# Activation differences made one kind at a time and in place, and a re-ordered start of the second MLP matrix, in a float32 transformer layer on one core

## The chip, the cores and the metric

The kernel runs on one core of one Trainium2 chip. The metric is the device time of one execution in microseconds. TensorE (PE) multiplies, VectorE (DVE) and ScalarE (ACT) work on tiles in on-chip memory, GpSimd (POOL) and SyncE (SP) mainly issue DMAs. Each engine carries out its instructions in the order of its own queue, and waits on semaphores for the others.

## The reference

The layer is an attention and gating part, then a squared-ReLU MLP; the change touches the MLP alone. Sequence 512, model width 2048, hidden width 8192, all float32.

```python
h2 = rms_norm(x, g_ff[l])
x = x + jnp.square(jax.nn.relu(h2 @ w_ff1[l])) @ w_ff2[l]
```

## The kernel before

**Three products for one.** Every operand is split into a part `hi` (the value cast to the matmul's type, a CAST on ScalarE) and a part `lo` (the value minus `hi`, a subtraction on VectorE), and `mm3` (L71 to L73) multiplies hi by hi, lo and then lo by hi. `split_to` does it (L106 and L107).

**Seven products for eight.** Most of the MLP runs in Strassen's form. A block of weights has the quarters a = w11, w12, b = w21, w22; `Sums.parts` makes from them the left factors of seven products, named y11, y21, m7, m6, y22, m4, m5 (`NAMES`), by sums in place on VectorE (L172, L176, L178) and one accumulating DMA on POOL's queue that adds w22 onto w21 for m5 (L174). Each product's weights are then split into the pieces `w_hi` and `w_lo`, which share a ring of six buffers: a piece can be written when TensorE is done with the one that lay there. The right factors are the activations' quarters y11, y21, y22 and the differences m7 = y12 - y22, m6 = m7 - y11, m4 = y21 + m6, m5 = y11 - y12, which `factors` makes in slots of their own; `halves` splits each into a hi and a lo half of one slot (`ys`). The products are summed in four PSUM banks (`BANK`): y11, m6 and m5 share a bank, m7 and m4 share one, and y21 and y22 have their own. Of the shared ones, the later product adds onto what lies there, after ScalarE has copied the earlier state out (L722) into the pair's activations `relu`; VectorE adds the others (L725).

**First matrix, w_ff1.** The hidden width is walked in 32 pairs p of 2 x 128 columns. Pairs 0 and 1 (`PLAIN`) are done without Strassen; in pair 1 all 32 differences of the input (`hs`, eight k of four kinds) are made. Pairs 2 to 31 are `strassen_columns`: 7 products x 8 k x 3 = 168 matmuls of 128x256. After each pair `keep_hidden` squares its activations, makes the same seven kinds of the hidden activations and stores them in DRAM (seven DMAs of 256 KB on SP's queue, `store`). The squares of pairs 0, 1 and 2 are all kept after pair 2.

**Second matrix, w_ff2.** Eight chunks f of four pairs, each in two halves g of the output columns (`strassen_tokens`, two sets of weights i per half, 168 matmuls of 128x512). The kept activations come back by 28 `fetch` DMAs per chunk on POOL's queue, those of the next chunk asked for between the products. The result is added onto the residual `x2`, sixteen tiles of 256 KB that are read back from `kept` after the last pair.

**Order.** The program is written in this order, and a scheduler places each engine's instructions by its own estimate of when they can start; so an engine's queue isn't the order of the text. TensorE's order within a pair is y11, y21, m7, y22, m6, m4, m5, in both kernels. `behind` is a list of pieces of work; `step` runs the next one, `flush` the rest.

Of the kernel before, what the change touches and what calls it, by code (L numbers as in the profile page):

```python
# [9 lines left out]
F32 = mybir.dt.float32  # L10
# [24 lines left out]
def tile_hybrid_layer(ctx: ExitStack, tc: tile.TileContext, x, g_mix, w_in, g_q, g_k, ln_g, ln_b,  # L35
# [17 lines left out]
    def slot(name, dt=F32, pool=slots):  # L53
        return pool.tile([P, 512], dt, name=name, tag="slot")
# [103 lines left out]
    class Sums:  # L158


        def __init__(self, blocks, tiles):

            self.blocks = blocks
            self.w11, self.w12, self.w21, self.w22, self.a, self.c = tiles
            for t, hc in ((self.w11, (0, 0)), (self.w12, (1, 0)), (self.w21, (0, 1)), (self.w22, (1, 1))):
                state["load"] = nc.sync.dma_start(out=t, in_=blocks[hc])
            self.take = {"y11": self.w11, "y21": self.w12, "m7": self.a, "m6": self.c, "y22": self.w12,
                         "m4": self.w22, "m5": self.w21}

        def parts(self, name):  # L170
            if name == "m7":
                nc.vector.tensor_tensor(out=self.a, in0=self.w11, in1=self.w21, op=ALU.add)  # L172

                nc.gpsimd.dma_start(out=self.w21, in_=self.blocks[1, 1], accum_op=ALU.add)  # L174
            if name == "m6":
                nc.vector.tensor_tensor(out=self.c, in0=self.a, in1=self.w22, op=ALU.add)  # L176
            if name == "y22":
                nc.vector.tensor_tensor(out=self.w12, in0=self.c, in1=self.w12, op=ALU.add)  # L178
            src = self.take[name]
            hi, lo = piece("w_hi"), piece("w_lo")  # L180
            like = "p (k c) -> p k c"
            hi, lo = (t.rearrange(like, k=src.shape[1]) for t in (hi, lo))
            split_to(hi, lo, src)
            return hi, lo

    def strassen_columns(wap, c0, rhs, evac):
# [4 lines left out]
        w = Sums(blocks, [state["raw"].tile([P, KH, P], F32, name="w_raw", tag="w_raw") for _ in range(6)])  # L191
# [12 lines left out]
    def strassen_tokens(wap, r0, c0, lhs, evac, between):  # L204

        KQ = 2
        ws = []
        for i in range(2):
            rows = wap[r0 + i * 2 * KQ * P:r0 + (i + 1) * 2 * KQ * P, :]
            blocks = {(h, c): rows[:, c0 + c * W:c0 + (c + 1) * W].rearrange("(k h p) c -> h p k c", p=P, h=2)[h]  # L210
                      for h in range(2) for c in range(2)}
            pool = (state["raw"], state["more"])[i]
            ws.append(Sums(blocks, [pool.tile([P, KQ, W], F32, name="w_raw", tag="w_raw") for _ in range(6)]))
        banks = {}
        for name in NAMES:
            b, new = BANK[name]
            if new:
                banks[b] = [(aux if b in (1, 3) else acc)("q") for _ in range(2)]
            for i in range(2):
                hi, lo = ws[i].parts(name)  # L220
                for t in range(2):
                    for k in range(KQ):
                        y = [part[:, t * P:(t + 1) * P] for part in lhs[name][i * KQ + k]]
                        mm3(banks[b][t], y, (hi[:, k, :], lo[:, k, :]), new and i == 0 and k == 0,
                            i == 1 and k == KQ - 1, skip_group_check=True)
            for t in range(2):
                evac(name, t, banks[b][t])
            between(name)


    warm = const.tile([P, 1], F32, name="warm")
# [406 lines left out]
    along(rstd2, rstd_b)  # L638


    def factors(ys, act, k):

        y11, y12, y21, y22 = act[0][:, :HS], act[0][:, HS:], act[1][:, :HS], act[1][:, HS:]
        ta, tb = slot("m"), slot("m")
        m = {"m7": ta[:, :HS], "m6": ta[:, HS:], "m4": tb[:, :HS], "m5": tb[:, HS:]}
        nc.vector.tensor_tensor(out=m["m7"], in0=y12, in1=y22, op=ALU.subtract)
        nc.vector.tensor_tensor(out=m["m6"], in0=m["m7"], in1=y11, op=ALU.subtract)
        nc.vector.tensor_tensor(out=m["m4"], in0=y21, in1=m["m6"], op=ALU.add)
        nc.vector.tensor_tensor(out=m["m5"], in0=y11, in1=y12, op=ALU.subtract)
        for name in ("m7", "m6", "m4", "m5"):  # L650
            ys[name, k] = halves(m[name])

    def halves(src, pool=slots):

        t = slot("ys", F32R, pool)
        split_to(t[:, :HS], t[:, HS:], src)
        return t
# [17 lines left out]
    chunks = DFF // (GROUP * 2 * P)  # L675
    store = [dram.tile([len(NAMES), GROUP, P, W], F32, name=f"store{f}") for f in range(chunks)]

    def keep_hidden(p, act):

        for a in act:  # L680
            nc.scalar.activation(out=a, in_=a, func=AF.Square)
        ys = {}
        for name, src in (("y11", act[0][:, :HS]), ("y21", act[1][:, :HS]), ("y22", act[1][:, HS:])):
            ys[name, 0] = halves(src)
        factors(ys, act, 0)
        for i, name in enumerate(NAMES):
            nc.sync.dma_start(out=store[p // GROUP][i, p % GROUP], in_=f32(ys[name, 0]))


    PLAIN = 2  # L690
# [1 line left out]
    for p in range(PLAIN):  # L692
        o = [acc("f1") for _ in range(2)]
        for kt in range(0, KT, 4):
            hi, lo = weight(w_ff1[0], kt, p * 2 * P, 2 * P)
            if p == PLAIN - 1:
                for k in range(kt // 2, kt // 2 + 2):
                    factors(hs, x2T[2 * k:2 * k + 2], k)
            for c in range(2):
                for k in range(4):  # L700
                    a = [part[:, k, c * P:(c + 1) * P] for part in (hi, lo)]
                    for half in range(2):
                        name = "y" + "12"[k % 2] + "12"[half]
# [8 lines left out]
    rhs = {name: [sides(hs[name, k]) for k in range(KT // 2)] for name in NAMES}  # L712

    def hidden(p):

# [11 lines left out]
        strassen_columns(w_ff1[0], p * 2 * P, rhs, evac)  # L727
        for a in act:
            nc.scalar.activation(out=a, in_=a, func=AF.Relu)
        return act  # L730
# [8 lines left out]
        return ts  # L739

    pairs = DFF // (2 * P)
    for p in range(PLAIN, pairs):
        acts.append(hidden(p))
        if p == pairs - 1:
            lhs = {name: fetch(0, name) for name in NAMES}
        while acts:
            keep_hidden(p + 1 - len(acts), acts.pop(0))

    first.close()
    state["more"] = ctx.enter_context(tc.tile_pool(name="more", bufs=6))  # L750
# [10 lines left out]
    done = {"y21": [(0, 0)], "m4": [(0, 1)], "m5": [(1, 1), (1, 0)]}  # L761
    for f in range(chunks):
        ahead = {}
        for g in range(2):
            def evac_y(name, t, o):
                for half, c, op in takes[name]:
                    a = x2[2 * half + t, 2 * g + c]
                    nc.vector.tensor_tensor(out=a, in0=a, in1=o, op=op)  # L768
                if f == chunks - 1:
                    for half, c in done.get(name, []):  # L770
                        tb, j = 2 * half + t, 2 * g + c
                        nc.sync.dma_start(out=out[tb * P:(tb + 1) * P, j * W:(j + 1) * W], in_=x2[tb, j])

            def between(name):

                i = NAMES.index(name) + g * 5
                if f < chunks - 1 and (i < 5 if g == 0 else i < 7):
                    ahead[NAMES[i]] = fetch(f + 1, NAMES[i])

            strassen_tokens(w_ff2[0], f * GROUP * 2 * P, g * 2 * W, lhs, evac_y, between)  # L780
        lhs = ahead


# [23 lines left out]
```

## Time and profile before

| what | us |
|---|---|
| time, median of 3 runs | 2529.26 (2526.61 to 2531.51) |
| the profiled execution, time | 2529.15 |
| the profiled execution, span | 2527.2 |
| attention, gating and the two plain pairs, to | 1270.9 |
| Strassen pairs 2 to 31 | 1270.9 to 1893.7 |
| token stage (w_ff2) | 1893.7 to 2521.5 |

The span is counted from the first to the last instruction of one profiled execution, and times in the views run from its start. In a row of the timeline the first number is the start, the second the duration, and the bracket behind it says how long the engine had been idle and what released it; matmuls overlap, so the distance of two starts is a matmul's cost, not its duration.

### The profile page before, as it was taken

To read this page: it belongs to the slowest core of one execution; us is meant where nothing else is said; L and a number is where in the kernel's file an instruction comes from. 1 tells how busy PE (TensorE), PEld (TensorE's weight loads), DVE (VectorE), ACT (ScalarE), POOL (GpSimd) and SP (SyncE) were. 2 spreads that over 40 slices of the span, in tenths; PEclk is the share of its full clock that TensorE was granted. 3 is DMA by queue.
4 is the path that set the end of the run, shared out by engine and by line. 5 is a ranking of instruction groups with operands and counts; after the bars stand their busy time and mean duration, and the time that the engine had idled before them with its cause. 6 is when DMAs were issued, how large, how long until landed. Compare 5 with 4: busy or idle time off the path is not lost.

```text
span 2527.2 us, 35103 instructions
## 1 busy us (share of the span) xinstructions
PE 2486.2 (98%) x13658; PEld 2170.2 (86%) x13658; DVE 1600.5 (63%) x2106; ACT 1036.0 (41%) x1510; POOL 336.7 (13%) x425
## 2 busy tenths in 40 slices
PE   8999999999999999999999999999988999999999
PEld 7888888888888888888889999999986888888887
DVE  4555463232335343332798888888877889889887
ACT  5333342222223322232466666666653333333333
POOL 0212110000121010100000000000033223222210
PEclk9999999999999999999999999999998999999999
DMA  5332322333433233344368888887899787777763
GB/s 175 92 84 75 92 67 92 100 96 97 117 93 108 92 96 120 117 158 125 85 185 220 229 227 223 220 223 214 221 313 332 248 257 248 223 215 221 248 183 94
DMA packets 324711, 418.62 MB, mean 166 GB/s; under 512 B 17040, under 2 KB 177856, under 8 KB 324544
## 3 DMA queue, kind: packets, MB, share of 16 engines
q1 hardware_dynamic: 265440, 320.94, 39.9%
q0 software_dynamic: 59104, 95.44, 15.9%
q8 instruction: 107, 1.75, 0.3%
q14 instruction: 60, 0.49, 0.1%
HBM read 349.20 MB, written 67.11 MB: 165 GB/s over the span
## 4 chain that ended last, share of the span: by engine, by line
PE 95%; DMA 2%; DVE 2%; issue 1%; ACT 1%; POOL 0%; SPq 0%; DVEq 0%; POOLq 0%; ACTq 0%
PE q L72 17%; PE q L71 17%; PE q L73 17%; PE xo L73 2%; PE xo L71 2%; PE xo L72 2%; PE gb L71 2%; PE gb L72 2%; PE gb L73 2%; PE ga L71 2%; PE ga L72 2%; PE ga L73 2%; DMA w_raw<-in_w_ff_dram 2%; PE v L71 1%; PE v L73 1%; PE v L72 1%
## 5 line engine op out<-in xcount | busy, mean ns | idle before, releaser
L106 ACT CAST w_hi<-w_raw 128x1024 fp32r<-128x1024 f32 x434 | 456.8, 1052 | 600.7 <-PE q L72 548.8
L95 DVE TENSOR_TENSOR w_lo<-w_raw,w_hi 128x1024 fp32r<-128x1024 f32 x216 | 268.1, 1241 | 597.2 <-ACT w_hi L93 593.0
L107 DVE TENSOR_TENSOR w_lo<-w_raw,w_hi 128x1024 fp32r<-128x1024 f32 x434 | 530.6, 1223 | 137.4 <-ACT w_hi L106 137.1
L93 ACT CAST w_hi<-w_raw 128x1024 fp32r<-128x1024 f32 x216 | 227.2, 1052 | 664.9 <-PE ga L72 99.6
L72 PE MATMUL q<-ys,w_hi 128*128 128x256 f32 x1680 | 476.4, 284 | 4.1 <-DVE ys L107 4.1
L73 PE MATMUL q<-ys,w_lo 128*128 128x256 f32 x1680 | 472.7, 284 | 6.4 <-DVE w_lo L107 6.4
L71 PE MATMUL q<-ys,w_hi 128*128 128x256 f32 x1680 | 476.7, 285 | 1.0 <-ACT ys L106 0.8
L72 PE MATMUL q<-w_lo,ys 128*128 128x512 f32 x896 | 351.3, 392 | 11.1 <-DVE w_lo L107 11.1
L73 PE MATMUL q<-w_hi,ys 128*128 128x512 f32 x896 | 350.8, 392 | 0.0
L72 PEld LDWEIGHTS q<-ys,w_hi 128*128 128x128 f32 x1680 | 324.5, 193 | 4.9 <-DVE ys L107 4.9
L73 PEld LDWEIGHTS q<-ys,w_lo 128*128 128x128 f32 x1680 | 322.4, 193 | 6.6 <-DVE w_lo L107 6.6
L71 PEld LDWEIGHTS q<-ys,w_hi 128*128 128x128 f32 x1680 | 324.5, 193 | 1.9 <-ACT ys L106 1.5
L71 PE MATMUL q<-w_hi,ys 128*128 128x512 f32 x896 | 315.3, 391 | 0.9 <-ACT w_hi L106 0.9
L72 PEld LDWEIGHTS q<-w_lo,ys 128*128 128x128 f32 x896 | 169.6, 189 | 47.5 <-DVE w_lo L107 12.2
L71 PEld LDWEIGHTS q<-w_hi,ys 128*128 128x128 f32 x896 | 169.5, 189 | 36.6 <-ACT w_hi L106 1.3
L73 PEld LDWEIGHTS q<-w_hi,ys 128*128 128x128 f32 x896 | 169.6, 189 | 35.4
L174 POOL DMA_DIRECT2D w_raw<-in_w_ff_dram x62 | 85.9, 1393 | 819.2 <-DVE w_raw L172 543.6
L768 DVE TENSOR_TENSOR x<-x,q 128x512 f32<-128x512 f32 x256 | 167.9, 682 | 9.0 <-PE q L73 7.3
L737 POOL DMA_DIRECT2D ys<-store x224 | 126.8, 599 | 208.0 <-PE q L73 173.1
L71 PE MATMUL xo<-w_hi,mT_hi 128*128 128x512 f32 x256 | 100.5, 393 | 0.0
L73 PE MATMUL xo<-w_hi,mT_lo 128*128 128x512 f32 x256 | 99.9, 391 | 0.0
L72 PE MATMUL xo<-w_lo,mT_hi 128*128 128x512 f32 x256 | 99.7, 389 | 0.0
(259 smaller groups left out, 4216.2 us busy)
## 6 DMA issues: line engine op xcount, KB each, us to landing
w_raw<-in_w_ff_dram SPq DMA_DIRECT2D x256, 512.0 KB, 5.2
w_raw<-in_w_in_dram SPq DMA_DIRECT2D x144, 512.0 KB, 3.8
store<-ys SPq DMA_DIRECT2D x224, 256.0 KB, 5.1
ys<-store POOLq DMA_DIRECT2D x224, 256.0 KB, 6.0
w_raw<-in_w_ff_dram POOLq DMA_DIRECT2D x62, 512.0 KB, 6.9
w_raw<-in_w_out_dram SPq DMA_DIRECT2D x32, 512.0 KB, 3.8
w_raw<-in_w_oa_dram SPq DMA_DIRECT2D x16, 512.0 KB, 3.7
w_raw<-in_w_ob_dram SPq DMA_DIRECT2D x16, 512.0 KB, 3.7
```

Source lines behind the costliest of these rows:

```text
L71: nc.tensor.matmul(o, lhsT=lh[0], rhs=rh[0], start=start, stop=False, **kw)
L72: nc.tensor.matmul(o, lhsT=lh[0], rhs=rh[1], start=False, stop=False, **kw)
L73: nc.tensor.matmul(o, lhsT=lh[1], rhs=rh[0], start=False, stop=stop, **kw)
L93: nc.scalar.copy(out=hi, in_=raw)
L95: nc.vector.tensor_tensor(out=lo, in0=raw, in1=f32(hi), op=ALU.subtract)
L106: nc.scalar.copy(out=hi, in_=src)
L107: state["lo"] = nc.vector.tensor_tensor(out=lo, in0=src, in1=f32(hi), op=ALU.subtract)
L174: nc.gpsimd.dma_start(out=self.w21, in_=self.blocks[1, 1], accum_op=ALU.add)
L737: nc.gpsimd.dma_start(out=f32(t), in_=store[f][NAMES.index(name), p])
L768: nc.vector.tensor_tensor(out=a, in0=a, in1=o, op=op)
```

## The change

- `factors` becomes `factor`, which makes one kind of difference, in place: m7, m6 and m4 in turn overwrite the quarter y22, and m5 overwrites y12. In the plain pair 1, m7 and m6 of the input are made; m4 and m5 follow as pieces of `behind`, run by the new `step()` behind each product of the first Strassen pair. `Late` looks a difference up only when its product asks for it.
- `keep_hidden` becomes `keeping`, a list of seven pieces that are run one after the other; a kind is stored as soon as it is made. The pieces of pair 31 go into `behind` when chunk f = 1 begins.
- In pair 31 and in chunk 0 (`loaded=False`), b + w22 is summed by VectorE (L181 after) in place of the accumulating DMA.
- The residual's reads are spread in eighths over the fetches of chunk 0 and its products, and the fetches of chunk 1 start later.

```diff
-                nc.gpsimd.dma_start(out=self.w21, in_=self.blocks[1, 1], accum_op=ALU.add)
+                if self.loaded:
+                    nc.gpsimd.dma_start(out=self.w21, in_=self.blocks[1, 1], accum_op=ALU.add)
...
+            if name == "m5" and not self.loaded:
+                nc.vector.tensor_tensor(out=self.w21, in0=self.w21, in1=self.w22, op=ALU.add)
...
-    def factors(ys, act, k):
+    def factor(ys, act, k, name):
...
-        ta, tb = slot("m"), slot("m")
-        m = {"m7": ta[:, :HS], "m6": ta[:, HS:], "m4": tb[:, :HS], "m5": tb[:, HS:]}
-        nc.vector.tensor_tensor(out=m["m7"], in0=y12, in1=y22, op=ALU.subtract)
-        nc.vector.tensor_tensor(out=m["m6"], in0=m["m7"], in1=y11, op=ALU.subtract)
-        nc.vector.tensor_tensor(out=m["m4"], in0=y21, in1=m["m6"], op=ALU.add)
-        nc.vector.tensor_tensor(out=m["m5"], in0=y11, in1=y12, op=ALU.subtract)
-        for name in ("m7", "m6", "m4", "m5"):
-            ys[name, k] = halves(m[name])
+        o, in0, in1, op = {"m7": (y22, y12, y22, ALU.subtract), "m6": (y22, y22, y11, ALU.subtract),
+                           "m4": (y22, y21, y22, ALU.add), "m5": (y12, y11, y12, ALU.subtract)}[name]
+        nc.vector.tensor_tensor(out=o, in0=in0, in1=in1, op=op)
+        ys[name, k] = halves(o)
...
-    def keep_hidden(p, act):
-
-        for a in act:
-            nc.scalar.activation(out=a, in_=a, func=AF.Square)
+    def keeping(p, act):
+
         ys = {}
-        for name, src in (("y11", act[0][:, :HS]), ("y21", act[1][:, :HS]), ("y22", act[1][:, HS:])):
-            ys[name, 0] = halves(src)
-        factors(ys, act, 0)
-        for i, name in enumerate(NAMES):
-            nc.sync.dma_start(out=store[p // GROUP][i, p % GROUP], in_=f32(ys[name, 0]))
+
+        def keep(name):
...
+            else:
+                factor(ys, act, 0, name)
+            nc.sync.dma_start(out=store[p // GROUP][NAMES.index(name), p % GROUP], in_=f32(ys[name, 0]))
+
+        return [lambda name=name: keep(name) for name in ("y11", "y21", "y22", "m7", "m6", "m4", "m5")]
...
-                for k in range(kt // 2, kt // 2 + 2):
-                    factors(hs, x2T[2 * k:2 * k + 2], k)
+                for i in range(kt, kt + 4):
+                    factor(hs, x2T[i % 8 * 2:i % 8 * 2 + 2], i % 8, "m7" if i < 8 else "m6")
...
+    behind.extend([lambda k=k: two(k) for k in range(1, KT // 2, 2)])
...
-    for p in range(PLAIN, pairs):
+    for p in range(PLAIN, pairs - 1):
         acts.append(hidden(p))
-        if p == pairs - 1:
-            lhs = {name: fetch(0, name) for name in NAMES}
+        flush()
         while acts:
-            keep_hidden(p + 1 - len(acts), acts.pop(0))
-
+            for keep in keeping(p + 1 - len(acts), acts.pop(0)):
+                keep()
+    act = hidden(pairs - 1)
...
+    def residual(half, t, c):
+        tb, j = 2 * half + t, c
+        x2[tb, j] = slot("x2")
+        nc.gpsimd.dma_start(out=x2[tb, j], in_=kept[tb, j])
+
+    lhs = {}
+    for name in NAMES:
+        lhs[name] = fetch(0, name)
+        if name in ("y11", "m7", "m6", "y22"):
+            half, c = {"y11": (0, 0), "m7": (1, 1), "m6": (0, 1), "y22": (1, 0)}[name]
+            for t in range(2):
+                residual(half, t, c)
     first.close()
     state["more"] = ctx.enter_context(tc.tile_pool(name="more", bufs=6))
-    for tb in range(NTB):
-        for j in range(D // W):
-            t = slot("x2")
-            nc.gpsimd.dma_start(out=t, in_=kept[tb, j])
-            x2[tb, j] = t
...
+        if f == 1:
+            behind.extend(keeping(pairs - 1, act))
```

ScalarE's queue in a Strassen pair in the middle of the stretch, before. `w_hi_13207`, `w_hi_13237` and `w_hi_13266` are the pieces of y22, m4 and m5; `ys` are halves of the pair that is being kept; `q_13088` is the bank of y11 (then m6, m5), `q_13150` that of m7 (then m4) and `q_13211` that of y22. The bracket names the engines and DMA queues that are waited for.

```order
L106 CAST w_hi_13207<-w_raw_13075 128x1024 [waits PE_49]
L106 CAST ys_13053<-m_13047 128x256 [waits DMAHW4_49,DVE_49]
L106 CAST ys_13056<-m_13047 128x256 [waits DMAHW5_49,DVE_49]
L106 CAST w_hi_13237<-w_raw_13077 128x1024 [waits DMAHW4_49,PE_49]
L106 CAST ys_13059<-m_13048 128x256 [waits DVE_49]
L106 CAST ys_13062<-m_13048 128x256 [waits DMAHW1_49]
L722 ACTIVATE relu_13072<-q_13088 128x256
L722 ACTIVATE relu_13073<-q_13150 128x256 [waits DMAHW2_49,PE_49]
L106 CAST w_hi_13266<-w_raw_13076 128x1024 [waits DMASW6_49,PE_49,Activation_49]
L722 ACTIVATE relu_13072<-q_13211 128x256 [waits PE_49]
```

The same place of the same pair in the changed kernel, from y22's piece on (`w_hi_13159`, m4's `w_hi_13189`, m5's `w_hi_13218`; the banks are `q_13040`, `q_13102`, `q_13163`):

```order
L106 CAST w_hi_13159<-w_raw_13027 128x1024 [waits PE_49]
L106 CAST ys_13005<-relu_12765 128x256 [waits DMAHW2_49,DVE_49]
L106 CAST w_hi_13189<-w_raw_13029 128x1024 [waits DMAHW4_49,PE_49]
L106 CAST ys_13010<-relu_12765 128x256 [waits DMAHW3_49,DVE_49]
L106 CAST w_hi_13218<-w_raw_13028 128x1024 [waits DMASW6_49,PE_49,Activation_49]
L106 CAST ys_13015<-relu_12765 128x256 [waits DVE_49]
L106 CAST ys_13020<-relu_12764 128x256
L753 ACTIVATE relu_13024<-q_13040 128x256
L753 ACTIVATE relu_13025<-q_13102 128x256 [waits DMAHW5_49]
L753 ACTIVATE relu_13024<-q_13163 128x256 [waits PE_49]
```

The cast of m5's piece now stands ahead of the copies of y11's and m7's banks, and the casts of the kept pair's m4 (`ys_13015`) and m5 (`ys_13020`) stand between them.

VectorE's queue at the same place of the changed kernel; the cast of `ys_13015` waits for the last of these rows, which makes m4 of the kept pair in place:

```order
L654 TENSOR_TENSOR relu_12765<-relu_12765,relu_12764 128x256 [waits DVE_49]
L107 TENSOR_TENSOR w_lo_13190<-w_raw_13029,w_hi_13189 128x1024 [waits PE_49,Activation_49]
L107 TENSOR_TENSOR ys_13010<-relu_12765,ys_13010 128x256 [waits DMAHW3_49,Activation_49]
L173 TENSOR_TENSOR w_raw_13290<-w_raw_13286,w_raw_13288 128x1024 [waits DMAHW3_49,DMAHW1_49,DVE_49]
L654 TENSOR_TENSOR relu_12765<-relu_12765 128x256 [waits DVE_49]
```

Before, m4 and m5 had slots of their own and were made ahead of m4's `w_lo`; now m4 can be made only when m6's halves have been read, and it stands behind that `w_lo` and the next pair's first sum (L173).

ScalarE's queue in pair 3 of the changed kernel, from m5's piece (`w_hi_9838`) to the copy of y11's bank (`q_9660`). `relu_9248`/`relu_9250` and `relu_9260`/`relu_9261` are the activations of pairs 1 and 2, which are being kept:

```order
L106 CAST ys_9591<-relu_9250 128x256 [waits DVE_49]
L106 CAST ys_9596<-relu_9250 128x256 [waits DVE_49]
L106 CAST ys_9601<-relu_9250 128x256 [waits DVE_49]
L106 CAST ys_9606<-relu_9248 128x256
L106 CAST ys_9612<-relu_9260 128x256 [waits DMAHW4_49]
L106 CAST ys_9616<-relu_9261 128x256 [waits DMAHW5_49]
L106 CAST ys_9620<-relu_9261 128x256 [waits DMAHW6_49]
L106 CAST ys_9625<-relu_9261 128x256 [waits DMAHW0_49,DVE_49]
L106 CAST ys_9630<-relu_9261 128x256 [waits DVE_49,Activation_49]
L106 CAST ys_9635<-relu_9261 128x256 [waits DVE_49,Activation_49]
L106 CAST ys_9640<-relu_9260 128x256 [waits DMAHW4_49]
L753 ACTIVATE relu_9644<-q_9660 128x256 [waits DMAHW5_49]
```

The row ahead of these is the cast of `w_hi_9838`. The three casts that read `relu_9250` after a subtraction, and the three of `relu_9261`, are links of the in-place chains of two kept pairs; all eleven stand ahead of the copy of y11's bank.

More of the change, by code (lines that the diff above doesn't have):

```diff
@@ L158, in tile_hybrid_layer, with __init__ @@
     class Sums:
-        def __init__(self, blocks, tiles):
-            self.blocks = blocks
+        def __init__(self, blocks, tiles, loaded=True):
+            self.blocks, self.loaded = blocks, loaded
             self.w11, self.w12, self.w21, self.w22, self.a, self.c = tiles
@@ L190, in strassen_columns @@
                   for h in range(2) for c in range(2)}
-        w = Sums(blocks, [state["raw"].tile([P, KH, P], F32, name="w_raw", tag="w_raw") for _ in range(6)])
+        w = Sums(blocks, [state["raw"].tile([P, KH, P], F32, name="w_raw", tag="w_raw") for _ in range(6)],
+                 loaded)
         banks = {}
@@ L202, in strassen_columns, with strassen_tokens @@
             evac(name, o)
-    def strassen_tokens(wap, r0, c0, lhs, evac, between):
+            step()
+    def strassen_tokens(wap, r0, c0, lhs, evac, between, loaded=True):
         KQ = 2
@@ L212, in strassen_tokens @@
             pool = (state["raw"], state["more"])[i]
-            ws.append(Sums(blocks, [pool.tile([P, KQ, W], F32, name="w_raw", tag="w_raw") for _ in range(6)]))
+            ws.append(Sums(blocks, [pool.tile([P, KQ, W], F32, name="w_raw", tag="w_raw") for _ in range(6)],
+                           loaded))
         banks = {}
@@ L228, in strassen_tokens @@
             between(name)
+            step()
     warm = const.tile([P, 1], F32, name="warm")
@@ L676, in tile_hybrid_layer @@
     store = [dram.tile([len(NAMES), GROUP, P, W], F32, name=f"store{f}") for f in range(chunks)]
-    def keep_hidden(p, act):
-        for a in act:
-            nc.scalar.activation(out=a, in_=a, func=AF.Square)
+    def keeping(p, act):
         ys = {}
-        for name, src in (("y11", act[0][:, :HS]), ("y21", act[1][:, :HS]), ("y22", act[1][:, HS:])):
-            ys[name, 0] = halves(src)
-        factors(ys, act, 0)
-        for i, name in enumerate(NAMES):
-            nc.sync.dma_start(out=store[p // GROUP][i, p % GROUP], in_=f32(ys[name, 0]))
+        def keep(name):
+            if name == "y11":
+                for a in act:
+                    nc.scalar.activation(out=a, in_=a, func=AF.Square)
+            if name in ("y11", "y21", "y22"):
+                h = act[name[1] == "2"]
+                ys[name, 0] = halves(h[:, :HS] if name[2] == "1" else h[:, HS:])
+            else:
+                factor(ys, act, 0, name)
+            nc.sync.dma_start(out=store[p // GROUP][NAMES.index(name), p % GROUP], in_=f32(ys[name, 0]))
+        return [lambda name=name: keep(name) for name in ("y11", "y21", "y22", "m7", "m6", "m4", "m5")]
     PLAIN = 2
@@ L711, in tile_hybrid_layer, with last_factors, __init__, __getitem__ @@
         acts.append(act)
-    rhs = {name: [sides(hs[name, k]) for k in range(KT // 2)] for name in NAMES}
+    def last_factors(k):
+        for name in ("m4", "m5"):
+            factor(hs, x2T[2 * k:2 * k + 2], k, name)
+    class Late:
+        def __init__(self, name):
+            self.name = name
+        def __getitem__(self, k):
+            return sides(hs[self.name, k])
+    rhs = {name: Late(name) for name in NAMES}
+    last_factors(0)
+    def two(k):
+        last_factors(k)
+        if k + 1 < KT // 2:
+            last_factors(k + 1)
+    behind.extend([lambda k=k: two(k) for k in range(1, KT // 2, 2)])
     def hidden(p):
@@ L725, in evac @@
                 nc.vector.tensor_tensor(out=a, in0=a, in1=o, op=op)
-        strassen_columns(w_ff1[0], p * 2 * P, rhs, evac)
+        strassen_columns(w_ff1[0], p * 2 * P, rhs, evac, loaded=p < pairs - 1)
         for a in act:
@@ L774, in between @@
             def between(name):
-                i = NAMES.index(name) + g * 5
-                if f < chunks - 1 and (i < 5 if g == 0 else i < 7):
+                i = NAMES.index(name)
+                if f == 0:
+                    for half, c in {(0, "m4"): [(0, 2)], (1, "y11"): [(1, 3)], (1, "y21"): [(0, 3)],
+                                    (1, "m7"): [(1, 2)]}.get((g, name), []):
+                        for t in range(2):
+                            residual(half, t, c)
+                    i = i - 6 if g == 0 else i + 1
+                    asked = 0 <= i < len(NAMES)
+                else:
+                    i += g * 5
+                    asked = i < (5 if g == 0 else 7)
+                if f < chunks - 1 and asked:
                     ahead[NAMES[i]] = fetch(f + 1, NAMES[i])
-            strassen_tokens(w_ff2[0], f * GROUP * 2 * P, g * 2 * W, lhs, evac_y, between)
+            strassen_tokens(w_ff2[0], f * GROUP * 2 * P, g * 2 * W, lhs, evac_y, between,
+                            loaded=f > 0)
         lhs = ahead
```

2 lines of the change are left out of this document (1 added, 1 removed).

## The prediction

> **What bounds the kernel now.** I read the page's first lines and its chain first, then the busy time by stretch.
>
> ```profile
> span 2527.2 us, 35103 instructions
> PE 2486.2 (98%) x13658; PEld 2170.2 (86%) x13658; DVE 1600.5 (63%) x2106; ACT 1036.0 (41%) x1510; POOL 336.7 (13%) x425
> PE 95%; DMA 2%; DVE 2%; issue 1%; ACT 1%; POOL 0%; SPq 0%; DVEq 0%; POOLq 0%; ACTq 0%
> ```
>
> TensorE is busy for 98% of the span and is 95% of the chain. Neither VectorE nor ScalarE bounds the kernel; they matter only where a matmul waits for them. So the sum counts TensorE stalls that go and stalls that come. The stretches (us, busy time of PE, PEld, DVE, ACT, POOL with instruction counts, granted clock, DMA share, GB/s) say where they are:
>
> ```profile
> 1276.00:1293.00 17.00, 11.96 (x62) 10.20 (x61) 16.96 (x44) 12.34 (x32) 0.11 (x1) 0.70 0.36 111
> 1300.00:1860.00 560.00, 560.00 (x4669) 560.00 (x4669) 474.38 (x700) 359.24 (x614) 42.80 (x29) 1.00 0.84 226
> 1880.00:1910.00 30.00, 18.67 (x88) 16.03 (x87) 17.13 (x22) 9.20 (x14) 13.87 (x23) 0.77 1.06 364
> 1910.00:1950.00 40.00, 32.94 (x128) 26.07 (x127) 26.78 (x34) 12.13 (x15) 16.48 (x28) 0.87 1.02 362
> ```
>
> From 1300 to 1860 there is nothing to gain: 560.00 of 560 us, 4669 matmuls at 560 / 4669 = 0.12 us, so a pair of 168 matmuls takes 20.16 us. Stalls stand in two places only: in pair 2, where 62 matmuls worth 62 x 0.12 = 7.4 us took 17 us (**9.6 lost**), and where the token stage begins, where TensorE idles 11.3 + 7.1 = 18.4 us, partly followed by a lower clock. The change touches both, and the pairs between.
>
> **The quiet stretch: ScalarE's queue.** TensorE runs a pair in the order y11, y21, m7, y22, m6, m4, m5. m6 adds onto the bank that held y11, so its first matmul waits for ScalarE's copy of y11 out of that bank (L722 before, L753 after). The rows of ScalarE in the section on the change show what is new: before, this copy and that of m7 stand ahead of the conversion of m5's weights; after, they stand behind it and two more casts. That is so in pairs 4 to 31, 28 of them. What the conversion of m5's weights waits for is seen in one pair of before, on ScalarE and then on TensorE:
>
> ```profile
> 1612.15 1.05 ACT L106 CAST w_hi<-w_raw 128x1024 fp32r<-128x1024 f32 x1 [1.00 <-PE q L72]
> 1613.10 0.71 ACT L106 CAST ys<-m 128x256 fp32r<-128x256 f32 x2
> 1613.72 0.65 ACT L722 ACTIVATE relu<-q 128x256 f32<-128x256 f32 x2
> 1615.07 1.05 ACT L106 CAST w_hi<-w_raw 128x1024 fp32r<-128x1024 f32 x1 [0.71 <-ACT relu L722]
> ```
>
> ```profile
> 1614.71 0.28 PE L72 MATMUL q<-ys,w_hi 128*128 128x256 f32 x1
> 1614.83 0.28 PE L73 MATMUL q<-ys,w_lo 128*128 128x256 f32 x1
> 1614.95 0.28 PE L71 MATMUL q<-ys,w_hi 128*128 128x256 f32 x1
> ```
>
> y22's 24 matmuls end where m6's first one starts, at 1614.95. The cast at 1615.07 is m5's. The releaser named, L722, had ended 0.7 us earlier; what ended just then is y22's last L72, at 1614.71 + 0.28 = 1614.99, which frees the buffer that the cast writes. So this cast cannot start before y22 is over, and in the changed order y11's copy starts later still, while m6 wants to start at 1614.95. From ScalarE's rows alone: 1615.07, plus 0.95 (a cast to its successor, 1612.15 to 1613.10), plus 2 x 0.31 for the casts of m4 and m5 of the kept pair (two took 0.71, one 0.40), plus 0.38 for the copy, plus 0.08 of handover (1614.99 to 1615.07) gives 1617.10: **2.15 us** of stall. VectorE makes it longer, since the cast of m4 needs the subtraction L654, which is queued behind a w_lo, a small lo and L173:
>
> ```profile
> 1613.23 1.23 DVE L107 TENSOR_TENSOR w_lo<-w_raw,w_hi 128x1024 fp32r<-128x1024 f32 x1 [0.39 <-ACT w_hi L106]
> 1614.38 0.75 DVE L107 TENSOR_TENSOR ys<-m,ys 128x256 fp32r<-128x256 f32 x2
> 1615.38 1.22 DVE L172 TENSOR_TENSOR w_raw<-w_raw 128x1024 f32<-128x1024 f32 x1
> 1616.51 1.22 DVE L107 TENSOR_TENSOR w_lo<-w_raw,w_hi 128x1024 fp32r<-128x1024 f32 x1
> ```
>
> 1614.38 + 0.33 (one small row before the next: two took 0.75, the last of them 0.42) + 1.13 (1615.38 to 1616.51) + 0.42 (the subtraction) + 0.08 = 1616.34 for the cast of m4; two casts to 1616.96, the copy to 1617.34, handover to 1617.42. That is **2.47 us**. The later of the two paths decides; I take 2.45, bounds 2.1 and 2.7. 28 x 2.45 = 68.6 us. Nothing hides it: this stretch has no idle TensorE time.
>
> **The clock after such a stall.** The granted clock (column before the DMA share) follows the stretch before it, as two neighbouring stretches of 3.41 us show, with three matmuls of the first, and two of another half-clock stretch:
>
> ```profile
> 1916.77:1920.18 3.41, 1.74 (x7) 0.88 (x7) 1.93 (x3) 1.04 (x1) 1.86 (x4) 1.00 1.04 411
> 1920.18:1923.59 3.41, 3.41 (x10) 2.63 (x9) 2.17 (x4) 0.00 (x0) 1.74 (x5) 0.50 1.04 407
> ```
>
> ```profile
> 1918.58 0.50 PE L71 MATMUL q<-w_hi,ys 128*128 128x512 f32 x1 [0.91 <-ACT w_hi L106]
> 1919.84 0.52 PE L72 MATMUL q<-w_lo,ys 128*128 128x512 f32 x1 [0.76 <-DVE w_lo L107]
> ```
>
> ```profile
> 1289.17 0.41 PE L73 MATMUL q<-ys,w_lo 128*128 128x256 f32 x1
> 1289.39 0.41 PE L71 MATMUL q<-ys,w_hi 128*128 128x256 f32 x1
> ```
>
> Idle times of 0.91 and 0.76 us in one stretch (busy 1.74 of 3.41) brought 0.50 in the next. At that clock a 256-wide matmul takes 0.215 instead of 0.12, so a full stretch costs 3.41 x (1 - 0.12 / 0.215) = 1.5 us. A stall of 2.45 start to start is about 2.3 us of idle time (0.16 us of it is the last matmul draining), enough if at least 1.67 of it falls into one stretch. Would it, in each pair? 20.16 + 2.45 = 22.61 us; seven stretches are 7 x 3.413 = 23.89. The difference, 1.28, lies inside what a half-clock stretch costs (0 to 1.5, less where the stall's tail reaches into it). A pair that starts later in its stretch pays less and the next one starts earlier, so I estimate that stall and stretch lock onto each other, one slow stretch per pair: 28 x 1.28 = 35.8 us. Bounds: 0 and 28 x 1.5 = 42.
>
> The Trainium skill, "TensorE: Matmul & The Clock Gate", section "HAM oscillation — how this bites in real kernels", gives the rule as "no PE-idle gaps >~3.4µs". By that rule a gap of 2.45 us keeps the full clock and this term would be 0. The rows at 1916.77 and 1920.18 speak against it: there two gaps under 1 us sufficed.
>
> **Pair 2.** Its waits, us in total, times, longest:
>
> ```profile
> PE q L72 <- DVE ys L107: 4.1, 3, 1.6
> PE q L71 <- ACT ys L106: 0.8, 2, 0.6
> ```
>
> Before, all 32 activation differences and their halves are made in the second plain pair, and m4's are not ready in pair 2. After, m7's and m6's are made first and m4's and m5's behind pair 2's steps, so those waits end: -9.6 (0 to -9.6). The same VectorE rows, pulled into the plain pairs, delay a weight half there now and then: +2 (0 to 4).
>
> **Pair 3.** Three pairs' keeping is queued at once. As the rows of ScalarE show, y11's copy stands behind m5's cast and eleven more casts; six of them hang on an in-place chain subtract, cast, lo, subtract. From y22's end: cast 1.05, w_lo 1.23, L654 0.42, L177 1.23, sixteen small VectorE rows x 0.33 = 5.3, four casts that nothing covers, each with two handovers (0.40 + 0.16), 2.2, the last two casts and the copy 1.1: 12.5, and 1.5 for a slow stretch: +14 (10 to 17).
>
> **Start of the token stage.** Waits of TensorE from 1880 to 1945, and two pieces of the chain:
>
> ```profile
> PE q L72 <- DVE w_lo L107: 11.1, 3, 5.4
> PE q L73 <- DVE w_lo L107: 6.4, 1, 6.4
> ```
>
> ```profile
> 1876.28 22.70 DMA w_raw<-in_w_ff_dram
> 1921.53 19.64 DMA w_raw<-in_w_ff_dram
> ```
>
> The load asked for at 1876.28 lands at 1898.98 among the fetches, and I see nothing that lands it sooner: the five accumulating DMAs of 512 KB that go are replaced at once by the next fetches in POOL's queue. The added L181 rows (five x 1.14 us) stand with both L177 ahead of the first w_lo of w_ff2, so the first column of f=0 waits for that load whole: the first two stalls stay about as long together (-1 to +3). The second load stood behind the last pair's seven stores of 256 KB, which the change takes out of SP's queue; the 5.4 us stall it ended goes, with about 1.5 us of slow clock. I take -8 for the place; bounds -20 (all idle time and part of the slow clock) and +5 (the stall stays and the sums cost their own time). The last pair's seven stores and eleven VectorE rows later lie beside TensorE's work of the first two chunks, where VectorE has room (26.78 of 40 us busy from 1910 to 1950), and cost 0; with no room each VectorE row would cost its 0.33 to 1.2 us. The residual's sixteen loads move between the fetches, the same bytes in the same queue, and cost 0 as long as VectorE's additions to it come after them.
>
> **The sum.** Profiled execution 2529.15 (the median is 2529.26): -9.6 + 2 + 14 + 68.6 + 35.8 - 8 = +102.8, **2632**.
>
> **Rivals.**
> - Stall without the slow clock, by mechanism: a single stall must empty a whole stretch before the clock drops. 2529.15 - 9.6 + 2 + 12.5 + 68.6 - 8 = 2595. For it: no isolated gap of this length exists in the quiet stretch to look at. Against it: the rows at 1916.77. A part of the pairs slow gives something between.
> - Only the steady stall is absent, since m5's cast finds a buffer that was freed before y22: 2529.15 - 9.6 + 2 + 14 - 8 = 2528, no change. Against it: the start at 1615.07, just after 1614.99.
> - Faster: ScalarE's copy of y11 is nowhere late. It decides whether that copy starts before about 1614.5 in the pair above; if so in pair 3 too, 2529.15 - 9.6 + 2 - 8 = 2513.5. Against it: the queue's rows, which a queue cannot overtake. The change would then do what it says in both places and nothing else.
> - The change doesn't do its part at the token stage (loads as late as before, POOL as full): the forecast plus 8, 2640.
>
> **How the numbers follow.** Forecast (with the last rival) 0.64; stall with no or few slow stretches 0.22; no change 0.04; faster 0.10, so slower by over 0.2% 0.86. About 0.2% is what a measurement of this kernel can tell from no change. The range takes the first two: from 2595 less 7 for a 2.2 us stall, 2588, to 2632 plus 28 x 0.2 of stall, 6 of clock and 8 at the token stage, 2652.
>
> **What would show it.** In the profile after: TensorE's idle time before L71 of q, with ScalarE's copy of relu as the releaser, about 28 times 2.3 us plus once 12; pairs 4 to 31 at a mean clock near 0.93 (one stretch in seven at 0.50) and 23.9 us each; 22.6 us at a clock of 1.00 would be the first rival. No wait for ys in pair 2. One stall fewer in the token stage. The prediction is wrong at its root if pairs still take 20.16 us.

## The result and the profile after

| | before | changed |
|---|---|---|
| time, median | 2529.18 us (2526.61 to 2531.51, 5 runs) | 2632.02 us (2630.48 to 2634.41, 5 runs) |
| ratio, 95% interval | | 1.0407 (1.0392 to 1.0423) |
| span of the profiled execution | 2527.2 us | 2628.8 us |

The change makes the kernel 4.1% slower. The first lines and the chain on the changed kernel's page:

```profile
span 2628.8 us, 35071 instructions
PE 2522.6 (96%) x13658; PEld 2203.0 (84%) x13658; DVE 1610.8 (61%) x2111; ACT 1035.8 (39%) x1510; POOL 331.1 (13%) x420
PE 88%; DVE 4%; ACT 3%; DMA 3%; issue 3%; POOL 0%; DVEq 0%; SPq 0%; ACTq 0%; POOLq 0%
```

The number of matmuls is the same and TensorE is still 96% busy, but its share of the chain fell from 95% to 88%, and VectorE and ScalarE, 3% together before, now hold 7%. A busy share that falls by two points hides this. TensorE's waits show it; the three longest from 1225 to 2100 us, with engine, line, releaser, then us in total, times, longest:

```profile
PE q L71 <- ACT relu L753: 79.2, 29, 13.8
PE q L72 <- DVE w_lo L107: 8.9, 4, 6.8
PE q L71 <- ACT w_hi L106: 0.7, 1, 0.7
```

The first line is new, and is the copy that the prediction named: 29 waits for the copy of y11's bank, one in each of the pairs 3 to 31: 13.8 us in pair 3, 60.3 us in the 27 pairs 4 to 30, and 5.1 us in pair 31. The others are what is left of pair 2's and the token stage's waits. The same by stretch (us, busy time of PE, PEld, DVE, ACT, POOL with counts, granted clock, DMA share, GB/s), first where pair 2 stalled before, then pairs 4 to 30:

```profile
1276.00:1293.00 17.00, 16.34 (x137) 16.14 (x136) 16.26 (x30) 11.70 (x28) 1.57 (x1) 1.00 0.63 160
1329.59:1974.60 645.01, 584.74 (x4538) 579.26 (x4537) 465.50 (x677) 348.12 (x594) 45.25 (x35) 0.94 0.71 190
```

Pair 2 is mended: 137 matmuls where there were 62. But 27 pairs now take 645.01 / 27 = 23.89 us each instead of 20.16, at a mean clock of 0.94 instead of 1.00. The starts of each part's first matmul in the two traces (for the last row, to the start of the last matmul) give the balance from the plain pairs on, in us:

| part | before | changed | difference | predicted |
|---|---|---|---|---|
| plain pairs 0 and 1 | 48.20 | 49.47 | +1.3 | +2 |
| pair 2 | 30.11 | 21.08 | -9.0 | -9.6 |
| pair 3 | 20.16 | 36.49 | +16.3 | +14 |
| pairs 4 to 30 | 544.32 | 645.01 | +100.7 | 27 x 3.73 = 100.7 |
| pair 31 and chunk 0 | 123.13 | 115.57 | -7.6 | 3.73 - 8 = -4.3 |
| chunks 1 to 7 | 532.89 | 532.89 | 0.0 | 0 |

One of the 27 pairs, on ScalarE, VectorE and TensorE:

```profile
1648.81 1.05 ACT L106 CAST w_hi<-w_raw 128x1024 fp32r<-128x1024 f32 x1 [1.53 <-PE q L72]
1649.76 0.40 ACT L106 CAST ys<-relu 128x256 fp32r<-128x256 f32 x1
1651.73 1.04 ACT L106 CAST w_hi<-w_raw 128x1024 fp32r<-128x1024 f32 x1 [1.57 <-issue]
1652.95 0.71 ACT L106 CAST ys<-relu 128x256 fp32r<-128x256 f32 x2 [0.17 <-DVE relu L654]
1653.57 0.93 ACT L753 ACTIVATE relu<-q 128x256 f32<-128x256 f32 x3
```

```profile
1651.03 0.42 DVE L107 TENSOR_TENSOR ys<-relu,ys 128x256 fp32r<-128x256 f32 x1
1651.36 1.22 DVE L173 TENSOR_TENSOR w_raw<-w_raw 128x1024 f32<-128x1024 f32 x1
1652.50 0.42 DVE L654 TENSOR_TENSOR relu<-relu 128x256 f32<-128x256 f32 x1
```

```profile
1651.49 0.28 PE L73 MATMUL q<-ys,w_lo 128*128 128x256 f32 x1
1654.00 0.39 PE L71 MATMUL q<-ys,w_hi 128*128 128x256 f32 x1 [2.23 <-ACT relu L753]
```

y22's last matmul starts at 1651.49, m6's first at 1654.00 instead of 1651.61: a stall of 2.39 us start to start (the distance of the two starts, less the 0.12 us of one matmul). ScalarE sits idle for 1.57 us ahead of m5's cast while y11's bank is long complete, and again 0.17 us for L654. The copy starts at 1653.57.

Pair 31 is unlike the others: its stall is 5.29 us. There the first sum that stands ahead of the kept m4's subtraction belongs to w_ff2, and it waits for a load; on VectorE and then on ScalarE:

```profile
1988.77 1.23 DVE L173 TENSOR_TENSOR w_raw<-w_raw 128x1024 f32<-128x1024 f32 x1 [2.81 <-DMA w_raw<-in_w_ff_dram]
1989.92 0.42 DVE L654 TENSOR_TENSOR relu<-relu 128x256 f32<-128x256 f32 x1
```

```profile
1990.37 0.71 ACT L106 CAST ys<-relu 128x256 fp32r<-128x256 f32 x2 [3.07 <-DVE relu L654]
```

The clock behind the stall, in two of the pairs 4 to 30: the stretch of 3.41 us that holds the stall, and the next one.

```profile
1651.43:1654.84 3.41, 1.18 (x10) 0.98 (x10) 3.41 (x7) 2.59 (x6) 1.56 (x1) 1.00 0.82 280
1654.84:1658.25 3.41, 3.41 (x19) 3.41 (x18) 1.35 (x2) 0.00 (x0) 0.00 (x0) 0.50 1.05 169
1627.53:1630.94 3.41, 1.59 (x14) 1.39 (x12) 3.41 (x5) 1.67 (x4) 0.25 (x1) 1.00 1.05 350
1630.94:1634.36 3.42, 3.00 (x25) 3.00 (x26) 2.61 (x5) 0.91 (x4) 1.32 (x1) 1.00 0.67 160
```

In the first pair the whole stall lies in one stretch (TensorE busy 1.18 of 3.41 us), and the next runs at 0.50. In the second its tail reaches into the next stretch (busy 1.59), and the clock stays at 1.00. Of the 27 pairs, 23 have the slow stretch: in them at most 0.32 us of the stall reaches into the next stretch. In the four that have none it is 0.37 to 0.42 us. A pair with the slow stretch takes about 24.1 us, one without 22.65.

### The profile page after: what moved, and what is told of

The parts are those of the page before. It is cut to its first block, busy times and chain, and to the rows that moved or that the text cites. A ratio compares the mean times of both kernels' runs of the same rounds, so it can differ in the third digit from the quotient of the medians.

```text
span 2628.8 us, 35071 instructions
## 1 busy us (share of the span) xinstructions
PE 2522.6 (96%) x13658; PEld 2203.0 (84%) x13658; DVE 1610.8 (61%) x2111; ACT 1035.8 (39%) x1510; POOL 331.1 (13%) x420
## 4 chain that ended last, share of the span: by engine, by line
PE 88%; DVE 4%; ACT 3%; DMA 3%; issue 3%; POOL 0%; DVEq 0%; SPq 0%; ACTq 0%; POOLq 0%
PE q L71 15%; PE q L72 15%; PE q L73 15%; PE xo L73 2%; PE xo L72 2%; DMA w_raw<-in_w_ff_dram 2%; PE xo L71 2%; PE gb L71 2%; PE gb L73 2%; PE gb L72 2%; PE ga L71 2%; PE ga L72 2%; PE ga L73 2%; ACT w_hi L106 1%; PE v L71 1%
## 5 line engine op out<-in xcount | busy, mean ns | idle before, releaser
L71 PE MATMUL q<-ys,w_hi 128*128 128x256 f32 x1680 | 495.6, 296 | 79.9 <-ACT relu L753 79.2
L72 PE MATMUL q<-ys,w_hi 128*128 128x256 f32 x1680 | 491.5, 293 | 0.0
L73 PE MATMUL q<-ys,w_lo 128*128 128x256 f32 x1680 | 486.8, 293 | 0.0
L71 PEld LDWEIGHTS q<-ys,w_hi 128*128 128x128 f32 x1680 | 340.7, 203 | 86.0 <-ACT relu L753 85.1
L72 PEld LDWEIGHTS q<-ys,w_hi 128*128 128x128 f32 x1680 | 341.1, 203 | 0.0
L73 PEld LDWEIGHTS q<-ys,w_lo 128*128 128x128 f32 x1680 | 338.3, 203 | 0.0
L175 POOL DMA_DIRECT2D w_raw<-in_w_ff_dram x57 | 79.4, 1393 | 886.5 <-DVE relu L654 593.9
```

The costliest lines, as they stand in the source:

```text
L71: nc.tensor.matmul(o, lhsT=lh[0], rhs=rh[0], start=start, stop=False, **kw)
L72: nc.tensor.matmul(o, lhsT=lh[0], rhs=rh[1], start=False, stop=False, **kw)
L73: nc.tensor.matmul(o, lhsT=lh[1], rhs=rh[0], start=False, stop=stop, **kw)
```

## The experiments

**Is it the order on ScalarE? Own slots for the kept differences.** Only the keeping is changed, back to slots of its own.

```diff
...
+            if name == "m7":
+                ta, tb = slot("m"), slot("m")
+                own.update(m7=ta[:, :HS], m6=ta[:, HS:], m4=tb[:, :HS], m5=tb[:, HS:])
...
-                factor(ys, act, 0, name)
+                in0, in1, op = {"m7": (y12, y22, ALU.subtract), "m6": (own["m7"], y11, ALU.subtract),
+                                "m4": (y21, own["m6"], ALU.add), "m5": (y11, y12, ALU.subtract)}[name]
+                nc.vector.tensor_tensor(out=own[name], in0=in0, in1=in1, op=op)
+                ys[name, 0] = halves(own[name])
```

> The changed kernel, but the kept pairs' four differences go into slots of their own again, as before; the input's are still made in place, and the start of the token stage is as changed. If the steady stall comes from ScalarE's order (y11's copy behind m5's cast and the kept m4's), which here is as before in pairs 4 to 31, the stall and its half-clock stretches go: 28 x 3.73 = 104 us less, and pair 3's stall shrinks to about 7 us: 2632 - 104 - 8 = 2520 us, between 2512 and 2526. If another part of the change slows the pairs (the differences of the input looked up late, the step behind each product), the pairs stay at 23.9 us and the time above 2600.

Measured: 2520.18 us, ratio to before 0.9963 (0.9948 to 0.9978). Pairs 4 to 30 take 544.32 us again, pair 3 28.67 us. The two longest of TensorE's waits that are left before the token stage, from 1225 to 1340:

```profile
PE q L71 <- ACT relu L761: 5.2, 1, 5.2
PE q L71 <- ACT w_hi L106: 0.8, 1, 0.8
```

So the steady stall belongs to the kept differences made in place, and with the rest of the change the kernel is 0.4% faster than before. It does not yet tell whether the data dependence or only the queue's order is the cause.

**Which row holds the copy? The copy queued ahead of m5's cast.**

```diff
         for name in NAMES:
-            hi, lo = w.parts(name)
+            with tc.issue_after(state["copy", "y11"].ins) if name == "m5" else nullcontext():
+                hi, lo = w.parts(name)
...
```

`state["copy", "y11"]` is the copy's instruction. ScalarE's rows in the middle of the stretch are now, by the queue's order (not a profile):

```
L106 CAST ys_13010<-relu_12765 128x256 [waits DMAHW3_49,DVE_49]
L106 CAST ys_13015<-relu_12765 128x256 [waits DVE_49]
L106 CAST ys_13020<-relu_12764 128x256
L754 ACTIVATE relu_13024<-q_13040 128x256
L754 ACTIVATE relu_13025<-q_13102 128x256 [waits DMAHW5_49,PE_49]
L754 ACTIVATE relu_13024<-q_13163 128x256 [waits PE_49]
L106 CAST w_hi_13218<-w_raw_13028 128x1024 [waits DMASW6_49,Activation_49]
```

> The changed kernel with one edge more: m5's cast is queued behind the copy of y11's bank, the casts of the kept m4 and m5 stay ahead of the copy. If m5's cast (which waits for the end of y22) is what holds the copy, the steady stall goes and the time falls to about 2530. If the path through VectorE holds it (w_lo of m4, a small lo, L173, the subtraction L654, then the two casts), the copy still starts about 2.4 us after y22's end, and the time stays at 2632, between 2625 and 2638.

Measured, one execution: 2625.85 us. TensorE's waits from 1330 to 1980, in this kernel and then in the changed one:

```profile
PE q L71 <- ACT relu L754: 60.7, 27, 2.7
```

```profile
PE q L71 <- ACT relu L753: 60.3, 27, 2.2
```

ScalarE in one pair of this kernel (L655 is the changed kernel's L654):

```profile
1696.95 0.71 ACT L106 CAST ys<-relu 128x256 fp32r<-128x256 f32 x2 [2.79 <-DVE relu L655]
1697.57 0.92 ACT L754 ACTIVATE relu<-q 128x256 f32<-128x256 f32 x3
1698.37 1.05 ACT L106 CAST w_hi<-w_raw 128x1024 fp32r<-128x1024 f32 x1
```

The same 27 waits, though m5's cast is out of the way: pairs 4 to 30 take 645.28 us instead of 645.01. (The profiled spans differ by 4.7 us, 2.7 of it in pair 3 and 1.5 in pair 31 and chunk 0.) The path through VectorE suffices: the cast of the kept m4 waits for the subtraction, and the copy stands behind it.

**The other path alone. The kept m4's subtraction ahead of the next pair's first sum.** Here m5's cast stays ahead of the copy and the VectorE path is made shorter, for pairs 5 to 30. `state["m4"]` collects the kept pairs' m4 subtractions.

```diff
         for name in NAMES:
-            hi, lo = w.parts(name)
+            late = name == "m7" and c0 >= 5 * 2 * P
+            with tc.issue_after(state["m4"][-2].ins) if late else nullcontext():
+                hi, lo = w.parts(name)
...
```

> The changed kernel with one edge more, for pairs 5 to 30: VectorE's first sum of the next pair (L173) is queued behind the kept pair's m4 subtraction, so the path through VectorE is some 1.1 us shorter and ScalarE's own path, which starts at y22's end with m5's cast, is the later one. By the prediction's rows the stall shrinks from 2.47 to 2.15 (measured 2.39, so about 2.1) and doesn't go. The clock: the changed kernel's profile shows a half-clock stretch behind each stall that left about 2.05 us or more without matmuls in one stretch of 3.41 us, and none behind four that left a little less. With a stall of 2.1 us a pair takes 22.3 us, 6.52 stretches, so the stall falls wholly into one stretch in at most about 4 pairs of 10: 27 x 0.3 less stall and 27 x (0.7 to 1.3) less clock, 2588 to 2604. If every stall of some 2 us brings its half-clock stretch, as in the changed kernel, 2622. If m5's cast holds nothing (only VectorE's path did), the stall falls to about 1.3 us and the time to 2560.

Measured, one execution: 2627.24 us. ScalarE and then TensorE in one pair:

```profile
1651.75 1.04 ACT L106 CAST w_hi<-w_raw 128x1024 fp32r<-128x1024 f32 x1 [1.57 <-issue]
1652.70 0.71 ACT L106 CAST ys<-relu 128x256 fp32r<-128x256 f32 x2
1653.32 0.92 ACT L757 ACTIVATE relu<-q 128x256 f32<-128x256 f32 x3
```

```profile
1651.51 0.28 PE L73 MATMUL q<-ys,w_lo 128*128 128x256 f32 x1
1653.74 0.38 PE L71 MATMUL q<-ys,w_hi 128*128 128x256 f32 x1 [1.95 <-ACT relu L757]
```

The idle 0.17 us ahead of the kept casts is gone, and ScalarE's own path alone sets the stall: matmuls start 2.23 us apart instead of 0.12, a stall of 2.11 us, where 2.1 was expected. So each of the two paths holds the copy by itself. The clock part of the expectation failed. Of the 27 pairs 4 to 30, 25 still have their slow stretch and take 23.86 us each, the other two 22.4; together they take 641.23 us. I had reckoned with the length of a pair without its slow stretch (22.3 us, 6.5 stretches). With it a pair takes 23.86 us, which is 6.99 stretches, so a stall that once fell into one stretch falls into nearly the same place of the seventh one after.

**In place, but another order.** The kept m4 and m5 are written behind the next pair's first two products.

```diff
-            for keep in keeping(p + 1 - len(acts), acts.pop(0)):
-                keep()
+            ks = keeping(p + 1 - len(acts), acts.pop(0))
+            for keep in ks[:5]:
+                keep()
+            behind.extend(ks[5:])
-    act = hidden(pairs - 1)
+    act = hidden(pairs - 1)
+    flush()
```

> The changed kernel, kept differences in place as changed, but the kept pair's m4 and m5 are written behind the next pair's first two products, so that the copy of y11's bank stands ahead of their casts in ScalarE's queue in pairs 4 to 31. If the order of the queue is the cause, the pairs run in 20.16 us although the differences are made in place: 2632 - 100 - 5 (pair 3) = 2527, between 2515 and 2540. If making them in place is the cause as such (a serial chain on VectorE and ScalarE), the pairs stay near 23.9 us and the time above 2600.

Measured, one execution: 2525.85 us. ScalarE in one pair, from the cast of the kept m6 on (the third row is the cast of m5's weights), and the stretch from 1330 to 1860:

```profile
1615.87 0.40 ACT L106 CAST ys<-relu 128x256 fp32r<-128x256 f32 x1
1616.18 0.38 ACT L753 ACTIVATE relu<-q 128x256 f32<-128x256 f32 x1
1617.85 1.05 ACT L106 CAST w_hi<-w_raw 128x1024 fp32r<-128x1024 f32 x1 [1.29 <-issue]
```

```profile
1330.00:1860.00 530.00, 530.00 (x4419) 530.00 (x4418) 449.96 (x660) 339.00 (x578) 40.94 (x27) 1.00 0.83 223
```

The differences are still made in place, the copy stands ahead of m5's cast and of the kept m4's, and TensorE is busy for all of 530 us. In pairs 4 to 30, which take 544.32 us as before, making them in place costs nothing as such; the order that the scheduler chose for it does. Why the scheduler's estimate led to that order, no run shows.

**The first part of the change alone, on the kernel before** (the input's differences one kind at a time and in place, `Late`, the steps behind the products):

```diff
...
-                for k in range(kt // 2, kt // 2 + 2):
-                    factors(hs, x2T[2 * k:2 * k + 2], k)
+                for i in range(kt, kt + 4):
+                    factor(hs, x2T[i % 8 * 2:i % 8 * 2 + 2], i % 8, "m7" if i < 8 else "m6")
...
+    behind.extend([lambda k=k: two(k) for k in range(1, KT // 2, 2)])
...
         acts.append(hidden(p))
+        flush()
```

> The kernel before with the first part of the change alone: the input's differences one kind at a time and in place, m4's and m5's behind the steps of pair 2; keeping and the start of the token stage as before. Pair 2 should lose its 9 us of stalls, the plain pairs should grow by about 1 us. If the keeping of pairs 0, 1 and 2, which is queued for pair 3, gives the gain back there (it took 8.5 us more in the kernel with own slots), the time is 2529 to 2531, no change. If that stall belongs to the other parts of the change, the time is 2521.

Measured: 2528.86 us, ratio 0.9998 (0.9989 to 1.0008). Its two stretches of pairs 2 and 3:

```profile
1270.00:1292.00 22.00, 21.18 (x177) 20.97 (x176) 22.00 (x45) 17.54 (x40) 1.57 (x1) 1.00 0.38 113
1292.00:1320.00 28.00, 22.47 (x177) 22.27 (x176) 22.75 (x40) 14.45 (x28) 1.55 (x1) 0.94 1.03 289
```

Pair 2 gains 8.9 us (21.24 instead of 30.11), pair 3 loses 7.1 (27.23) and the plain pairs 1.2. The gain moved one pair on and was lost there.

**Pair 3's stall: the keeping spread**, with own slots:

```diff
...
-        flush()
-        while acts:
-            for keep in keeping(p + 1 - len(acts), acts.pop(0)):
-                keep()
+        if p == PLAIN:
+            flush()
+        if len(acts) > 1:
+            while acts:
+                behind.extend(keeping(p + 1 - len(acts), acts.pop(0)))
+        else:
+            for keep in keeping(p, acts.pop(0)):
+                keep()
```

(and a `flush()` behind pair 31.)

> As the kernel with own slots, but the keeping of pairs 0 and 1 is spread behind the steps of pairs 3 and 4, and each later pair's keeping is written behind the next pair's products until the queue has caught up. If pair 3's stall of 5.3 us and its half-clock time come from three pairs' keeping ahead of the copy of y11's bank, pair 3 falls from 28.7 to 20.2 to 21.5 us and the time to 2512 (2510 to 2515), which beats both kernels. If the stall is only put off to pairs 4 to 6, the time stays at 2517 to 2521.

Measured: 2510.24 us, ratio 0.9927 (0.9912 to 0.9941), the fastest of all and 0.7% faster than before. From 1270 to 1880 the stretch is nearly without a stall:

```profile
1270.00:1880.00 610.00, 608.32 (x5064) 607.51 (x5062) 522.63 (x783) 391.93 (x684) 56.29 (x52) 1.00 0.83 229
```

Pairs 2 and 3 take 20.16 us each. The 8.5 us that pair 3 lost with own slots came from three pairs' keeping in front of one copy.

**The token stage: the last pair kept at once.** Own slots, but `keeping(pairs - 1, act)` is run right behind pair 31.

> As the kernel with own slots, but the last pair is kept at once, so that its seven stores of 256 KB stand in SP's queue ahead of the second column's loads again. If these stores were what made those loads late, TensorE's wait for w_lo near the second column of chunk 0 (5.4 us before) comes back, 5 to 9 us more than with own slots. If the later residual and fetches made the difference, the time is within 2 us of that kernel's.

Measured, one execution: 2531.86 us, 11.7 more than with own slots; the direction was right, the size above the 5 to 9 expected. TensorE's wait from 1920 to 1950, and the load that ends it (start and length of its piece of the chain), then the load asked for at the same time in the kernel with own slots:

```profile
PE q L72 <- DVE w_lo L107: 14.4, 1, 14.4
```

```profile
1916.52 23.56 DMA w_raw<-in_w_ff_dram
```

```profile
1916.65 15.08 DMA w_raw<-in_w_ff_dram
```

SyncE's queue in the kernel of this experiment has the seven stores ahead of six loads; with own slots it has ten loads in a row there, from 1890.59 on:

```profile
1900.90 4.90 SPq L703 DMA_DIRECT2D store<-ys  x7
1909.10 12.72 SPq L167 DMA_DIRECT2D w_raw<-in_w_ff_dram  x6
```

Behind the seven stores this load takes 8.5 us longer, and the wait of 14.4 us is longer than the one of before (5.4). The edit also brings forward the kept pair's rows on VectorE and ScalarE; how much of the 11.7 us is theirs is not shown, nor what the residual in eighths and the later fetches do by themselves.

**The token stage: accumulating DMAs again.** Own slots, with `loaded=True` throughout.

> As the kernel with own slots (2520), but the accumulating DMAs do the sum for m5 in the last pair and in chunk 0 as before, in place of VectorE's L181. If the VectorE sums, which stand ahead of chunk 0's first w_lo, cost their time there (two of 1.14 us), the time is 2 to 3 us less. If the five accumulating DMAs of 512 KB hold up the fetches and loads in the full queues, it is 2 to 8 us more. If both queues are full either way and VectorE has room, within 1.5 us.

Measured: 2521.39 us (2519.67 to 2522.28, 6 runs), 1.2 us above own slots and within the spread of both. The stall only moves: 30.95 us for pair 31 instead of 20.43, then 84.34 us for chunk 0 instead of 93.25.

## Why the prediction was right, step by step

- **The steady stall** (28 x 2.45 = 68.6 us): right in mechanism, place and size for 27 of the 28 pairs, where it is 2.39 us. The two paths worked out for it, 2.15 and 2.47, are both real: 2.11 us where ScalarE's path alone decides, 2.39 where VectorE's comes last. Pair 31 was sized wrongly: its stall is 5.29 us, because the first sum on its VectorE path belongs to w_ff2 and waits for a load, which the prediction did not reckon with. Removing the order, by own slots or by writing two pieces later, removes the stall.
- **The half-clock stretch** (28 x 1.28 = 35.8): right in sum. Half-clock stretches and stall together make the mean pair seven stretches long, so the length came out right although the stall was 0.06 us shorter than taken and the rest of the pair that much longer. The pairs without and with it differ by 24.13 - 22.65 = 1.48 us, 23 of 27 have it, and the mean pair is 23.89 us, as reckoned. The way there is not quite the one predicted: the stall does not settle where its tail shortens the slow stretch, it drifts by 0.24 us per pair until enough of it has left its stretch, and then one pair pays nothing. Nor is 1.67 us of idle time always enough: with 3.41 - 1.59 = 1.82 in one stretch the clock stayed full.
- **The rule on gaps.** By the Trainium skill, "TensorE: Matmul & The Clock Gate", section "HAM oscillation — how this bites in real kernels", no gap below some 3.4 us should have cost clock. The trace does not agree: gaps of 2.39 and 2.11 us, a single one in each pair, halved it in nearly every pair.
- **Pair 2** (-9.6, measured -9.0) and **the plain pairs** (+2, measured +1.3): right, the first shown by itself in the kernel with the first part alone.
- **Pair 3** (+14, measured +16.3): right in mechanism: own slots for the kept differences shorten its stall from 14.0 to 5.3 us, and the spread keeping removes the rest. The stall itself was 14.0 instead of 12.5, and slow clock took about 2.3 instead of 1.5.
- **The token stage** (-8): pair 31 and chunk 0 together came to -7.6 where -4.3 was predicted, which is -11.3 for this place if pair 31 is counted at its predicted 3.73. Its stall of 5.29 us lies beside the loads of this place, so how the sum splits between the two is not shown. The stores in front of the loads were named rightly; with them back the kernel with own slots is 11.7 us slower. That the sums on VectorE in place of DMAs change little there was right within 1.5 us.

The sum was +102.8 us, the spans differ by 101.6. The term for pair 3 was 2.3 us too small, and the sum for pair 31 and chunk 0 was 3.3 us too large; the two errors nearly cancel, and that the total agrees so closely is in part luck.

## What to carry to other kernels

An edit that saves buffers can cost through the order that a scheduler then gives an engine which is idle 60% of the time: look at what stands in its queue ahead of the one row for which the bounding engine waits, and multiply by the number of rounds. A short stall per round costs more than its length when it lowers the clock behind it. When a stall at the start of a loop goes, look for where the work that caused it is queued next.

## What the runs showed of the hardware

A stall of 2.1 to 2.4 us once per round, in rounds that take 22.4 to 22.65 us with it, is mostly followed by a half-clock stretch of 3.41 us that lengthens the round to about 7 x 3.41 = 23.9 us, and so stays in step with the stretches: 23 of 27 rounds in one kernel, 25 of 27 in another. A shorter stall (2.11 us) is then hardly cheaper than a longer one (2.39): 641.23 / 27 = 23.75 against 23.89 us per round. No single length of idle time in a stretch decides it here: where a boundary of the stretches cut the stall (start to start, less one matmul), 1.82 us on the longer side still brought the slow stretch in one pair, and 1.97 to 2.03 us did not in four others.
